# Ten gather buffers in place of six, and products eight slots behind their gathers, in the second group's layers

## The chip, the cores and the metric

The kernel runs on one core of a Trainium2 chip. The metric is the device time of one execution in microseconds, taken as the median of several runs. The core has five engines that run lists of instructions side by side: TensorE (PE in the profile, with its weight loads as PEld), VectorE (DVE), ScalarE (ACT), GpSimd (POOL) and SyncE (SP, which only issues transfers here). Data moves between memory and the core's buffers over 16 DMA engines, which all queues share.

## The reference

512 tokens of width 1024 go through five layers and a feed-forward part with experts ("peer"), all in float32:

```python
x = x + rmsnorm(mamba2_mixer(rmsnorm(x)))        # then sliding-window attention, a hybrid of
...                                              # delta rule and mLSTM, and cross attention
def peer_ffn(h, wq, sub_keys, u_table, v_table):
    q = (hf @ wq).reshape(t, PEER_HEADS, 2, PEER_HALF)
    sc = jnp.einsum('thpd,hpnd->thpn', q, sub_keys).astype(jnp.float32)
    top_v, top_i = lax.top_k(sc, PEER_TOPK)
...
    def block(args):
        xb, eb, gb = args
        u = jnp.take(u_table, eb, axis=0)
        act = jax.nn.gelu(jnp.einsum('phkd,pd->phk', u, xb).astype(jnp.float32), approximate=False)
        wgt = (gb * act).astype(v_table.dtype)
        return jnp.einsum('phk,phkd->pd', wgt, jnp.take(v_table, eb, axis=0))
```

Every token picks 8 x 16 = 128 of 16384 experts. An expert is one row of 1024 numbers in `u_table` and one in `v_table`. The chosen rows of u are multiplied with the token and summed, which gives 128 activations; the rows of v, weighted by these, are added to the token. At the end there is one more norm.

## The kernel before

The tokens are worked on in two groups of two blocks of 128 tokens. Group 0 goes through the five stages `mamba`, `swa`, `hybrid`, `cross` and `route` first (until about 780 us); `route` gives each of its tokens the list of 128 experts. Then group 1 goes through the same five stages, and its own experts are computed densely: `dense` builds a matrix of gates (`gate_matrix`) and then runs 128 steps over all 16384 experts, 128 at a time (`steps`). A word, `phase`, says where the program is in group 1: "B" in the four layers `mamba` to `cross`, "R" in `route`, "G" while the gates are built, "D" in the 128 steps.

Beside group 1's work, group 0's experts are done row by row. The class `Rows` holds a list of 512 gathers: for each of the two blocks 128 of u and then 128 of v. One gather is an indirect DMA that GpSimd issues (L1946): it fetches, for each of the 128 tokens of a block, one row of a table, into a buffer `gu` of 128 x 1024 numbers (512 KB). There are six such buffers (GBUF). `take()` makes the product that belongs to a gather on VectorE: for u, `gu` times the token, summed into one column of `act` (L1967); for v, `x` plus `gu` times a column of `act` (L1973). The products follow their gathers in a list `pend`: `next(lag)` issues a gather and, if more than `lag` are pending, one product. So with a lag of five a product stands five slots behind its gather.

Slots come from the main work. `run()` lets the main work pass from point to point, and at each point adds a rate (1.0 in "B" for `mamba`, 1.1 for the other layers, 0.5 in "R" and "G"); whenever the sum reaches one, the generator `after()` calls `rows.next(GLAG)` with a lag of five. In the dense steps `steps()` itself calls `rows.next(LAGD)`, with LAGD = 3, at a rate that uses up all that is left by the fifth step from the end. `behind()` ties each gather and product to the last matmul so far, for the order of instructions alone; it adds no waiting.

When the last product of a block has been made, `final()` norms the block: a square on ScalarE (L1856), a load of the norm's weights that ScalarE's queue issues (L1860), a product on VectorE (L1862) and the store, again from ScalarE's queue (L1863). For group 0 it stands in `ends`, and each call of `next` runs one half of it; what is left is run after the 128 steps by `drain()`. Group 1's two blocks come after that.

Two more tiles bear on the change. Layers of group 0 hold the low parts of split operands in a tile `hl` (pool `hp`) and a tile `ol` (pool `op`), each 128 x 2 x 1024 numbers or as large. In the layers of group 1 the products are made in full float32 without a split, so neither is in use there; `dense()` takes `hl` again at its start.

In a layer of group 1 the weights come over SP's queue (L359) into three tiles each of `wraw`, `whi` and `wlo`, and TensorE multiplies (L404, transposes L412). VectorE adds the evacuated parts to x (L646, L656), norms x (L500) and makes the products of the gathers between, all in the order of its list.

Of the kernel before, what the change touches and what calls it, by code (L numbers as in the profile page):

```python
# [9 lines left out]
F32 = mybir.dt.float32  # L10
# [10 lines left out]
D = 1024  # L21
# [138 lines left out]
GBUF = 6  # L160
HP = 99
WV = (2, 3)
GLAG = 5
GLEAD = 2
GD = 2.9
GU = 0.75
# [20 lines left out]
class Kern:  # L187
# [72 lines left out]
    @staticmethod  # L260
    def weave(main, side, ratio):
        acc = 0.0
        for _ in main:
            yield
            acc += ratio
            while side is not None and acc >= 1:
                acc -= 1
                if next(side, 0) == 0:
                    side = None
        if side is not None:  # L270
            for _ in side:
                yield
# [1138 lines left out]
    @staticmethod  # L1411
    def weave_keep(main, side, ratio):
        acc = 0.0
        for _ in main:
            yield
            acc += ratio
            while acc >= 1:
                acc -= 1
                next(side, 0)
# [289 lines left out]
    def gate_matrix(self, G, gd, gt):  # L1709
# [7 lines left out]
        acc = 0.0  # L1717
        for s in range(-GLEAD, n + 2):
            if 0 <= s - 2 and s % 2:
# [3 lines left out]
            if 0 <= s - 1 < n:  # L1723
# [5 lines left out]
                nc.scalar.copy(st[:, :, t0 % 8:t0 % 8 + 4, :], q4(p[:, :, 32:128]))  # L1729
            m = s + GLEAD  # L1730
            if m < n:
# [19 lines left out]
            while acc >= 1:  # L1751
                acc -= 1
                next(self.plain, 0)
# [162 lines left out]
    def after(self, gi, x, nb):  # L1916
        yield from self.tail
        self.tail = None
        self.rows = Rows(self, gi, x, nb, self.routed)
        while self.rows.seq:  # L1920
            self.rows.next(GLAG)
            yield
        self.rows.drain()


class Rows:
# [9 lines left out]
    def next(self, lag):  # L1936

        k = self.k
        if self.ends:
            if next(self.ends[0], 0) == 0:  # L1940
                self.ends.pop(0)
        if self.seq:
            b, v, s = self.seq.pop(0)
            t = k.gp.tile([128, D], F32, name="gu", tag="gu", bufs=GBUF)
            table = k.a["p_v" if v else "p_u"]
            self.behind(k.nc.gpsimd.indirect_dma_start(out=t, out_offset=None, in_=table,  # L1946
                                                       in_offset=bass.IndirectOffsetOnAxis(ap=self.res[b][0][:, s:s + 1], axis=0)))
            self.pend.append((b, v, s, t))
            if len(self.pend) > lag:
                self.take()  # L1950
        elif self.pend:
            self.take()

    def behind(self, inst):

        k = self.k
        if k.phase not in "GD":
            k.tc.add_manual_dep(inst.ins, k.last.ins.name, mybir.DependencyInfo(
                mybir.DependencyClass.NoSync, mybir.DependencyReason.SCHED_ONLY), reason="spread over the products")
# [97 lines left out]
```

## Time and profile before

| | us |
|---|---|
| Median of three runs | 2600.91 (2598.08 to 2602.4) |
| The profiled execution | 2595.71 |
| Its span in the profile | 2593.7 |
| TensorE busy | 2376.1 (92%) |
| TensorE weight loads busy | 2134.6 (82%) |
| VectorE busy | 1987.4 (77%) |
| ScalarE busy | 1170.7 (45%) |
| GpSimd busy | 1077.3 (42%) |

The shares are means over stages with different limits: a busy share says little of what one edit is worth, so the stages are looked at apart. The granted clock of TensorE is 0.963 of full speed on the mean. The queue of the gathers (software_dynamic) carried 268 MB of 642 MB. In the chain of work that ended last, TensorE has 60% of the span, VectorE 20%, GpSimd 6% and transfers 5%.

### The profile page before, as it was taken

The page shows a single profiled execution, that of the slowest core. Times are in us where ns is not written, and L with a number is a line of the kernel's source. Part 1 is how long each engine was busy: PE and PEld are TensorE (multiplying, and loading weights), DVE is VectorE, ACT ScalarE, POOL GpSimd, SP SyncE. Part 2 cuts the span into 40 slices and gives each one's busy share as a digit, 9 for nine tenths or more (in the row PEclk, how much of TensorE's full clock was granted, in tenths as well). Part 3 has the DMA queues.
Part 4 walks back from the last instruction along what each step waited for, and adds up shares of the span by engine and source line. Part 5 has one row for each costly group of instructions (what it writes and reads, how often), then busy time and mean ns, then how long its engine had stood idle before and what let it go on. Part 6 is the DMA issues. An engine that isn't in the chain of part 4 may idle for free.

```text
span 2593.7 us, 41054 instructions
## 1 busy us (share of the span) xinstructions
PE 2376.1 (92%) x14872; PEld 2134.6 (82%) x14872; DVE 1987.4 (77%) x3989; ACT 1170.7 (45%) x2406; POOL 1077.3 (42%) x910
## 2 busy tenths in 40 slices
PE   7999998998989899979799859999769999999997
PEld 7999898998988788868678848888658999999974
DVE  7787657757589887877698786794997777777776
ACT  6766566644545433333252312222565444444443
POOL 1112001231011776753568775324335555555552
PEclk9999999999989899989899979999999999999999
DMA  6555434325446999986888689877888888888874
GB/s 203 178 172 156 148 118 142 116 89 150 141 131 197 352 380 358 341 297 224 336 308 302 226 324 353 288 236 282 249 237 302 316 311 286 319 317 300 294 276 152
DMA packets 203962, 642.33 MB, mean 248 GB/s; under 512 B 21104, under 2 KB 53360, under 8 KB 202480
## 3 DMA queue, kind: packets, MB, share of 16 engines
q1 hardware_dynamic: 97216, 347.19, 40.1%
q0 software_dynamic: 73728, 268.47, 28.6%
q10 hardware_dynamic: 32816, 24.06, 2.9%
q8 instruction: 117, 1.92, 0.3%
q14 instruction: 85, 0.70, 0.1%
HBM read 621.74 MB, written 17.89 MB: 247 GB/s over the span
## 4 chain that ended last, share of the span: by engine, by line
PE 60%; DVE 20%; issue 6%; POOL 6%; DMA 5%; ACT 4%; ACTq 0%; POOLq 0%; DVEq 0%; SPq 0%
PE mm L404 37%; PE ax L404 17%; PE tp L404 3%; POOL gu L1946 3%; PE tp L412 2%; DVE x L1973 2%; DVE gu L1967 2%; DMA gu<-in_p_v,eid 2%; DVE wlo L379 2%; DVE cacc L532 1%; DVE o L1736 1%; DMA gu<-in_p_u,eid 1%; DVE q L1738 1%; DVE o L1743 1%; ACT whi L376 1%
## 5 line engine op out<-in xcount | busy, mean ns | idle before, releaser
L379 DVE TENSOR_TENSOR wlo<-wraw,whi 128x1024 fp32r<-128x1024 f32 x285 | 357.2, 1254 | 206.7 <-ACT whi L376 206.4
L1946 POOL DMA_INDIRECT gu<-in_p_v,eid x256 | 367.5, 1436 | 192.4 <-DVE x L1973 111.5
L1946 POOL DMA_INDIRECT gu<-in_p_u,eid x256 | 313.0, 1223 | 273.8 <-DVE gu L1967 171.7
L404 PE MATMUL mm<-hl,whi 128*128 128x256 f32 (+1 forms) x1376 | 392.0, 285 | 0.0
L376 ACT CAST whi<-wraw 128x1024 fp32r<-128x1024 f32 x285 | 298.9, 1049 | 183.9 <-PE mm L404 86.6
L1967 DVE SCALAR_TENSOR_TENSOR gu<-gu,hf 128x1024 f32<-128x1024 f32 x256 | 318.4, 1257 | 45.4 <-DMA gu<-in_p_u,eid 45.0
L1973 DVE SCALAR_TENSOR_TENSOR x<-gu,act,x 128x1024 f32<-128x1024 f32 x256 | 335.3, 1310 | 14.4 <-DMA gu<-in_p_v,eid 13.4
L404 PE MATMUL mm<-hh,whi 128*128 128x260 f32 (+1 forms) x1232 | 331.9, 345 | 2.7 <-DVE spp L563 1.5
L404 PE MATMUL mm<-hh,wlo 128*128 128x260 f32 (+1 forms) x1200 | 320.9, 340 | 4.1 <-DVE wlo L379 4.1
L404 PEld LDWEIGHTS mm<-hl,whi 128*128 128x128 f32 x1376 | 262.7, 191 | 5.0
L1809 POOL TENSOR_TENSOR w<-act,w 128x256 fp32r<-128x256 f32 x128 | 146.4, 1144 | 281.9 <-issue 218.1
L404 PEld LDWEIGHTS mm<-hh,whi 128*128 128x128 f32 x1232 | 237.4, 195 | 22.7 <-ACT hh L510 2.8
L404 PEld LDWEIGHTS mm<-hh,wlo 128*128 128x128 f32 x1200 | 232.8, 196 | 21.5 <-DVE wlo L379 5.0
L404 PE MATMUL mm<-dhh,wlo 128*128 128x256 f32 x752 | 211.7, 282 | 0.0
L404 PE MATMUL mm<-dhh,whi 128*128 128x256 f32 x752 | 209.8, 279 | 0.0
L404 PE MATMUL mm<-wlo,hh 128*128 128x256 f32 x656 | 176.6, 329 | 0.0
L404 PE MATMUL mm<-whi,hh 128*128 128x256 f32 x608 | 166.8, 328 | 0.4 <-ACT hh L510 0.4
L404 PE MATMUL mm<-whi,oh 128*128 128x256 f32 x560 | 147.5, 328 | 1.3 <-DVE ysb L646 1.1
L404 PE MATMUL mm<-hh,wraw 128*128 128x256 f32 (+1 forms) x608 | 147.1, 390 | 0.3 <-ACT act L1706 0.3
L1804 ACT CAST w<-act 128x256 fp32r<-128x256 f32 x128 | 52.2, 408 | 206.9 <-DVE act L1802 204.7
L404 PEld LDWEIGHTS mm<-dhh,whi 128*128 128x128 f32 x752 | 141.1, 188 | 4.0
L404 PEld LDWEIGHTS mm<-dhh,wlo 128*128 128x128 f32 x752 | 141.3, 188 | 0.0
(494 smaller groups left out, 5646.6 us busy)
## 6 DMA issues: line engine op xcount, KB each, us to landing
wraw<-in_w SPq DMA_DIRECT2D x238, 512.0 KB, 4.0
wraw<-in_p_v SPq DMA_DIRECT2D x78, 512.0 KB, 4.7
wraw<-in_p_ut SPq DMA_DIRECT2D x69, 512.0 KB, 4.6
whi<-in_w SPq DMA_DIRECT2D x55, 512.0 KB, 6.1
wlo<-in_w SPq DMA_DIRECT2D x55, 512.0 KB, 6.2
wrawd<-in_p_v SPq DMA_DIRECT2D x50, 512.0 KB, 4.8
wrawd<-in_p_ut SPq DMA_DIRECT2D x36, 512.0 KB, 4.4
gd<-gst ACTq DMA_DIRECT2D x32, 384.0 KB, 3.6
```

What stands on the lines that cost most here:

```text
L376: nc.scalar.copy(hi, raw)
L379: (nc.gpsimd if le == "P" else nc.vector).tensor_tensor(lo, raw, hi.bitcast(F32), op=ALU.subtract)
L404: inst = self.last = self.nc.tensor.matmul(out, lhsT, rhs, start=start, stop=stop, skip_group_check=True)
L412: return self.nc.tensor.transpose(out, in_, self.ident[:in_.shape[0], :in_.shape[0]])
L532: nc.vector.scalar_tensor_tensor(acc, ps[:, 1 + j:1 + j + gt], w[:, j:j + 1], acc, op0=ALU.mult, op1=ALU.add)
L1736: nc.vector.tensor_tensor(o1, self.iota4.rearrange("p i t -> p t i"), row(self.sTb[:, 0, :]), op=ALU.is_equal)
L1738: nc.vector.tensor_tensor(q, self.iota4, col(self.sTb[:, 1, :]), op=ALU.is_equal)
L1804: nc.scalar.copy(wt[:, 0:gt], act)
L1809: nc.gpsimd.tensor_tensor(wt[:, gt:2 * gt], act, wt[:, 0:gt].bitcast(F32), op=ALU.subtract)
L1946: self.behind(k.nc.gpsimd.indirect_dma_start(out=t, out_offset=None, in_=table, in_offset=bass.IndirectOffsetOnAxis(ap=self.res[b][0][:, s ...
L1967: self.behind(nc.vector.scalar_tensor_tensor(t, t, 1.0, self.hf[:, b, :], op0=ALU.mult, op1=ALU.mult, accum_out=acts[b][:, s:s + 1]))
L1973: self.behind(nc.vector.scalar_tensor_tensor(x[:, b, :], t, acts[b][:, s:s + 1], x[:, b, :], op0=ALU.mult, op1=ALU.add))
```

## The change

In phase "B" the lag is eight instead of five, and the gathers go round ten row buffers: the six `gu` buffers, then the two halves of a tile `hl`, then the two halves of a tile `ol`. Outside of phase "B" a gather takes a `gu` buffer as before. In `next`, `if` becomes `while`, so that as many products are made as it takes to bring the list down to the lag asked for.

```diff
@@ -161,6 +161,7 @@
 GLAG = 5
+DEEP = 8
 GLEAD = 2
...
@@ -1918,7 +1919,7 @@
         while self.rows.seq:
-            self.rows.next(GLAG)
+            self.rows.next(DEEP if self.phase == "B" else GLAG)
             yield
...
@@ -1941,15 +1942,28 @@
             b, v, s = self.seq.pop(0)
-            t = k.gp.tile([128, D], F32, name="gu", tag="gu", bufs=GBUF)
+            t = self.buf()
...
             self.pend.append((b, v, s, t))
-            if len(self.pend) > lag:
+            while len(self.pend) > lag:
                 self.take()
         elif self.pend:
             self.take()
+
+    def buf(self):
+
+        k = self.k
+        r = k.rot("rb", GBUF + 4) if k.phase == "B" else 0
+        if r < GBUF:
+            return k.gp.tile([128, D], F32, name="gu", tag="gu", bufs=GBUF)
+        if r % 2 == 0:
+            if r == GBUF:
+                self.pair = k.hp.tile([128, 2, D], F32, name="hl", tag="hl")
+            else:
+                self.pair = k.op_tile([128, 2, D], "ol", "ol")
+        return self.pair[:, r % 2, :]
```

Since lines are added, a line of the kernel after has a higher number: the gather is L1947, the products are L1981 and L1987, the final norm is L1857 to L1864, and the other lines quoted here are one higher.

GpSimd's list in the first layer of group 1, where the ring of buffers has gone round once, reads thus before. A row gives the line, the output and the inputs with numbers of their tiles, the size, and the counts on other engines' semaphores that the instruction waits for (DMASW0 to DMASW7 are eight semaphores of the gathers' queue).

```order
L1946 DMA gu_10246<-in_p_u,eid_9968 128x1024 [waits DMASW6_49,DVE_49]
L1946 DMA gu_10270<-in_p_u,eid_9968 128x1024 [waits DMASW7_49,DVE_49]
L1946 DMA gu_10284<-in_p_u,eid_9968 128x1024 [waits DMASW0_49,DVE_49]
L1946 DMA gu_10295<-in_p_u,eid_9968 128x1024 [waits DMASW1_49,DVE_49]
L1946 DMA gu_10303<-in_p_u,eid_9968 128x1024 [waits DMASW2_49,DVE_49]
L1946 DMA gu_10321<-in_p_u,eid_9968 128x1024 [waits DMASW3_49,DVE_49]
```

After the change the same place on GpSimd reads:

```order
L1947 DMA gu_10241<-in_p_u,eid_9968 128x1024 [waits DMASW6_49,DVE_49]
L1947 DMA gu_10265<-in_p_u,eid_9968 128x1024 [waits DMASW7_49,DVE_49]
L1947 DMA hl_10279<-in_p_u,eid_9968 128x1024 [waits DMASW0_49]
L1947 DMA hl_10279<-in_p_u,eid_9968 128x1024 [waits DMASW1_49]
L1947 DMA ol_10297<-in_p_u,eid_9968 128x1024 [waits DMASW2_49]
L1947 DMA ol_10297<-in_p_u,eid_9968 128x1024 [waits DMASW3_49]
L1947 DMA gu_10322<-in_p_u,eid_9968 128x1024 [waits DMASW4_49,DVE_49]
```

The gathers stand at the same places; four in ten now go to the halves of `hl` and `ol`, and in each round the waits on VectorE are fewer. The number in a wait's name isn't the product waited for.

VectorE's list at the end of the hybrid layer, where TensorE's last output parts are added to x and the next norm begins, reads thus before:

```order
L646 TENSOR_TENSOR x<-mm,x 128x256
L1967 SCALAR_TENSOR_TENSOR gu,act<-gu,hf 128x1024
L496 TENSOR_REDUCE ns_15326<-xss 128x1
L496 TENSOR_REDUCE ns_15335<-xss 128x1
L1967 SCALAR_TENSOR_TENSOR gu,act<-gu,hf 128x1024
L458 TENSOR_SCALAR nv<-ns_15326 128x1
L458 TENSOR_SCALAR nv<-ns_15335 128x1
L1967 SCALAR_TENSOR_TENSOR gu,act<-gu,hf 128x1024
L500 TENSOR_SCALAR xn<-x,nr 128x512 x4
```

After the change, at the same place on VectorE:

```order
L647 TENSOR_TENSOR x<-mm,x 128x256
L1981 SCALAR_TENSOR_TENSOR gu,act<-gu,hf 128x1024
L497 TENSOR_REDUCE ns_15265<-xss 128x1
L497 TENSOR_REDUCE ns_15274<-xss 128x1
L1981 SCALAR_TENSOR_TENSOR gu,act<-gu,hf 128x1024
L459 TENSOR_SCALAR nv<-ns_15265 128x1
L459 TENSOR_SCALAR nv<-ns_15274 128x1
L1981 SCALAR_TENSOR_TENSOR hl,act<-hl,hf 128x1024
L501 TENSOR_SCALAR xn<-x,nr 128x512 x4
```

The products stand at the same places, but each is that of a gather three slots older, and some read `hl` or `ol`.

ScalarE's list at the end of the program, in the last steps of the dense stage (`w` is a step's weighted activation, `whi` the high part of a weight tile), reads thus before:

```order
L376 CAST whid<-wraw 128x1024
L1804 CAST w<-act 128x256
L376 CAST whi<-wrawd 128x1024
L1804 CAST w<-act 128x256
L376 CAST whi<-wrawd 128x1024
L1804 CAST w<-act 128x256
L376 CAST whi<-wraw 128x1024
L1804 CAST w<-act 128x256
L376 CAST whid<-wraw 128x1024
L1856 ACTIVATE gu,fss<-x 128x1024
L1860 DMA gu<-in_bcw 128x1024
L1856 ACTIVATE gu,fss<-x 128x1024
```

After the change, the same stretch of ScalarE's list:

```order
L1805 CAST w<-act 128x256
L1857 ACTIVATE gu,fss<-x 128x1024
L1861 DMA gu<-in_bcw 128x1024
L377 CAST whid<-wraw 128x1024
L1805 CAST w<-act 128x256
L1864 DMA out<-gu 128x1024
L377 CAST whi<-wrawd 128x1024
L1805 CAST w<-act 128x256
L377 CAST whi<-wrawd 128x1024
L1805 CAST w<-act 128x256
L377 CAST whi<-wraw 128x1024
L1805 CAST w<-act 128x256
```

One square, one load of the norm's weights and one store have moved from behind the last step's casts to between them, four steps ahead of the end. The cause is the `while`: in the dense steps the lag asked for is three, the `if` kept the pending list at five there, and now it is brought to three.

## Rows read from the trace of the kernel before

**Rows 1.** Windows: us; PE, PEld, DVE, ACT, POOL busy; PEclk, DMA share, GB/s

```profile
835.00:1640.00 805.00, 707.18 (x3633) 606.62 (x3632) 639.61 (x1216) 260.90 (x635) 531.36 (x454) 0.92 0.87 319
...
1943.00:2480.00 537.00, 534.77 (x3406) 483.81 (x3405) 421.82 (x388) 258.98 (x387) 288.43 (x196) 1.00 0.87 306
2480.00:2594.00 114.00, 95.55 (x368) 64.59 (x366) 76.35 (x83) 42.77 (x64) 45.49 (x41) 0.95 0.58 199
```

**Rows 2.** Windows of the gathers' line alone: us, GpSimd's busy time and count

```profile
835.00:1640.00 805.00, 406.12 (x334) 0.92 0.87 319
1943.00:2480.00 537.00, 169.96 (x97) 1.00 0.87 306
```

**Rows 3.** Waits, 835 to 1640: who waited for whom: us, times, longest

```profile
POOL gu L1946 <- DVE x L1973: 72.0, 35, 7.7
POOL gu L1946 <- DVE gu L1967: 63.9, 49, 4.0
PE tp L412 <- DVE xn L500: 40.6, 7, 14.1
DVE gu L1967 <- DMA gu<-in_p_u,eid: 35.8, 36, 4.3
PE ax L404 <- DVE m_h L817: 14.4, 7, 4.8
DVE x L1973 <- DMA gu<-in_p_v,eid: 13.4, 19, 3.3
```

**Rows 4.** The gathers' line from 1520 to 1545: their count, and issue to landing

```profile
L1946 POOL DMA_INDIRECT gu<-in_p_u,eid x15: 935/937/1913, 1519.1 to 1544.2; - x15
...
DMA to landing us min/median/max: 6.6/8.8/10.5
```

**Rows 5.** Timeline, 1540 us: start, duration, instruction, [idle before <- releaser]

```profile
1540.57 1.24 DVE L1967 SCALAR_TENSOR_TENSOR gu<-gu,hf 128x1024 f32<-128x1024 f32 x1 [0.29 <-DMA gu<-in_p_u,eid]
...
1541.74 0.41 DVE L646 TENSOR_TENSOR x<-mm,x 128x256 f32<-128x256 f32 x1
...
1542.20 1.22 PE L404 MATMUL mm<-wraw,oh 128*128 128x256 f32 x3 [1.90 <-DVE x L646]
```

**Rows 6.** Timeline: the first and the last of the 13 gaps

```profile
938.31 1.22 DVE L1967 SCALAR_TENSOR_TENSOR gu<-gu,hf 128x1024 f32<-128x1024 f32 x1 [1.16 <-DMA gu<-in_p_u,eid]
...
940.20 0.43 PE L404 MATMUL ax<-xdt,M 128*128 128x64 f32 x2 [2.30 <-DVE M L788]
...
1631.20 1.23 DVE L1967 SCALAR_TENSOR_TENSOR gu<-gu,hf 128x1024 f32<-128x1024 f32 x1 [0.73 <-DMA gu<-in_p_u,eid]
...
1637.21 0.69 PE L412 MATMUL tp<-ident,xn 128*128 128x128 f32 x2 [1.25 <-DVE xn L500]
```

**Rows 7.** Windows, two stretches of the layers, columns as in rows 1

```profile
925.00:950.00 25.00, 20.82 (x107) 18.14 (x105) 21.92 (x47) 6.33 (x16) 20.09 (x16) 0.91 1.00 377
...
1530.00:1545.00 15.00, 12.14 (x48) 9.17 (x47) 11.35 (x21) 2.55 (x10) 7.61 (x9) 0.92 1.03 418
```

**Rows 8.** Timeline of GpSimd: a gather and the state step behind it

```profile
1021.97 1.68 POOL L1946 DMA_INDIRECT gu<-in_p_u,eid  x1 [2.51 <-DVE gu L1967]
...
1025.21 0.62 POOL L816 TENSOR_TENSOR m_h<-m_h,cde 128x256 f32<-128x256 f32 x1
```

**Rows 9.** Timeline of VectorE at the start of the route stage

```profile
1651.09 0.49 DVE L1522 MAX8 tv<-sc 128x8 f32<-128x128 f32 x2 [11.25 <-ACT sc L1570]
```

**Rows 10.** The gathers' line in the dense stage: issue to landing

```profile
DMA to landing us min/median/max: 4.6/6.6/11.3
```

**Rows 11.** Timeline of VectorE in the first dense step

```profile
1952.90 1.28 DVE L1973 SCALAR_TENSOR_TENSOR x<-gu,act,x 128x1024 f32<-128x1024 f32 x1
```

**Rows 12.** Timeline at the end, then the transfers of the norm's weights

```profile
2575.40 1.06 ACT L1856 ACTIVATE gu<-x 128x1024 f32<-128x1024 f32 x1
...
2588.20 1.28 DVE L1862 SCALAR_TENSOR_TENSOR gu<-x,finr,gu 128x1024 f32<-128x1024 f32 x1 [3.22 <-DMA gu<-in_bcw]
...
gu<-in_bcw ACTq DMA_DIRECT2D x5, 512.0 KB, 3.9
```

## The prediction

> **What bounds the kernel now.** I read the busy times by stage first [rows 1]. In the layers of the second group (835 to 1640 us) TensorE is busy 707 of 805 us, so 98 us are idle there; VectorE has 640 us of work and the transfer engines are taken 0.87 of the time. In the dense stage (1943 to 2480) TensorE is busy 534.8 of 537 us: nothing but its own work bounds that part. In the last 114 us it is busy 95.6. The gathers that the change speaks of lie mostly in the first of these stages, 334 of 512, and 97 stand in the dense stage [rows 2].
>
> Then I read what the idle engines of the layers wait for [rows 3]. A gather on GpSimd waits for the product that frees its buffer 72.0 + 63.9 = 135.9 us in all. That is the wait the words of the change name, but GpSimd is busy only 531 of 805 us. VectorE waits for a gather to land 35.8 + 13.4 = 49.2 us in 55 waits. This one can matter, since VectorE runs its list in order and a product that waits holds up whatever stands behind it. A product stands five slots behind its gather; 334 slots in 805 us are 2.4 us each, so five slots are about 12 us on the mean. From 1519.1 to 1544.2 us, though, 15 gathers start [rows 4], one every 1.8 us, and five slots are 9.0 us, while these gathers land after 6.6 / 8.8 / 10.5 us (least, median, most).
>
> What one such wait does is seen at 1540 us [rows 5]. The product at 1540.57 waited 0.29 us for its gather; only then could VectorE add the evacuated part at 1541.74, and TensorE, which needs that buffer, started at 1542.20 after 1.90 us of idleness. I went through all TensorE gaps of over 0.6 us in this stage for those with a VectorE wait for a gather in the 6 us ahead: 13 gaps, 36.9 us together. The first and the last of them are [rows 6]. Taking from each gap no more than the gather waits ahead of it (2.30 us with a wait of 1.64 summed over its 6 us at the first, 1.25 with 0.73 at the last) gives 13.2 us. Six lie outside the stretches where the transfers are full (1.64, 1.55, 0.64, 0.84, 0.94, 0.83: 6.4 us), seven inside (1.06, 0.62, 1.90, 0.59, 0.96, 0.92, 0.73: 6.8 us).
>
> **The change part by part.** The number of gathers, products and matmuls stays; no work is added.
>
> *Eight slots and ten buffers in the layers.* Eight slots at 1.8 us are 14.3 us, over the longest landing of 10.5 us [rows 4]. So a wait for a gather goes wherever the transfer engines have room. Where they have none, depth gives only three transfers ahead, once per stretch. The stretch 1530 to 1545 moves 418 GB/s at a share of 1.03 [rows 7]. I take the 6.4 us outside in full and half of the 6.8 us inside: **-9.8 us**. Bounds: nothing (the gap is then ended by the rest of the chain) and -13.2 by these gaps; -49.2 if every wait counted.
>
> Ten buffers do not give ten gathers in flight: as the listing of GpSimd shows, every gather from the ninth on also waits for one of eight semaphores in rotation, thus for the gather eight before it to have landed. After the change a gather waits for the product of ten before it, which stands two slots earlier; the wait for a product goes from GpSimd and the semaphore's takes part of its place. Eight gathers of 0.52 MB (128 rows of 4 KB) at 418 GB/s take 10.0 us if they had all the rate, so in full stretches the wait may just move from buffer to semaphore. That costs GpSimd nothing it doesn't pay now.
>
> The rate of 418 GB/s also bears on a rule. In the Trainium skill, DMA: Bandwidth & Descriptors, section Bandwidth, the measured rate of one core alone ends at 425 GB/s for large transfers, near the ceiling of its ports; the rows' 418 agrees with it. By that rule the 6.8 us inside full stretches would stay whole, and this term would be -6.4.
>
> *GpSimd's own steps.* A gather that waits holds up the state update behind it: at 1021.97 a gather starts after 2.51 us of waiting for a product, and the state step follows at 1025.21 [rows 8]. TensorE waits for that state 14.4 us in 7 waits [rows 3]. Bounds 0 and -14.4; I take **-1 us**, since the gather's own 1.7 us and the rest of the state's chain stay.
>
> *The clock.* In 925 to 950 and 1530 to 1545 the granted clock reads 0.91 and 0.92, a mean of stretches at 2.4 and some at 1.2 GHz, with TensorE idle for 4.2 and 2.9 us in them [rows 7]. At full clock their busy times would fall by at most 20.82 x 0.09 + 12.14 x 0.08 = 2.8 us. I take **-2 us**, bounds 0 and -2.8.
>
> *Layer boundaries.* TensorE waits 40.6 us in 7 waits for a normed x [rows 3]. That chain is the norm's; I count nothing for it, as its first and longest part follows the last matmul of a layer whatever the gathers do.
>
> *Route stage: a burst.* At the first slot of that stage the `while` brings nine pending down to five: three more products than now, about 3.8 us of VectorE work. VectorE waits 11.25 us for scores at 1651.09 [rows 9], which covers it: **0**. Uncovered it would be +3.8.
>
> *Dense stage: the lag falls to three.* Now the `if` takes one product for each gather, so five stay pending though the dense stage asks for three. The `while` brings it to three: two more products in the first dense slot (1.28 us each, the one there now is [rows 11]), 2.6 us of VectorE ahead of the first splits. VectorE is busy 421.8 of 537 us, so bounds 0 and +2.6; I take **+0.5**. From then on a product follows its gather by three slots of 537/97 = 5.5 us, 16.6 us, against landings of 6.6 in the median and 11.3 at most [rows 10]: no new wait.
>
> *End.* As the pending list is shorter by two, it empties two calls earlier, and the final norm of the first group's last block moves from behind the 128 steps into the last steps. There ScalarE and VectorE alternate in one chain: step's cast, split, next product. The listing of ScalarE shows the square, the load of the norm's weights and the store among the casts. The square is 1.06 us and the norm's product 1.28 us [rows 12], so 2.3 us on that chain; the store, on ScalarE's queue, waits for a norm whose weights take 3.9 us to land [rows 12] where a step is some 3.3 us, another 0.6. The tail loses as much work: the last norm now waits 3.22 us for its weights at 2588.20, and with two norms instead of three behind the last matmul up to 2.3 us go. Net +2.9 - 2.3 = +0.6; I take **+1**, bounds -2.3 (all hidden) and +6.2 (2.3 and the whole 3.9, none back).
>
> Sum: -9.8 - 1 - 2 + 0 + 0.5 + 1 = **-11.3 us**. The profiled execution took 2595.71 us (span 2593.7), so 2584.4 by it. That execution is 0.2% under the median of 2600.91; the same -0.435% of the median gives **2590 us**.
>
> **The rivals.**
>
> *No gain, about 2599 us.* The gaps stay, because they are ended by chains that have other waits just behind, or because the wait is for bandwidth and not for depth. For it: the full stretches at 418 GB/s [rows 7], and that TensorE's gaps in [rows 6] are longer than the waits ahead of them, so something else is in them. Against it: six of the gaps lie where transfers have room. With the full-stretch half whole and half of the other gone it is -3.2 - 1 + 1.5 = -2.7. In this case belong also the eight semaphores: if gathers in flight stay capped where they already are, the change does not do what its ten buffers say.
>
> *The larger gain, about 2576 us.* VectorE's lateness lasts beyond 6 us: a product that waits pushes all later adds and casts, and half of the 49.2 us comes back, -25. For it: 98 us of idle TensorE in the stage [rows 1]. Against: VectorE has slack (640 of 805) and catches up between.
>
> *Slower, about 2607 us.* The lag of three in the dense stage: +2.6 for two products at its start and +6.2 at the end with none given back, against a gain in the layers of 2 us or less: 8.8 - 2 = +6.8. It decides as soon as the layers give back less than 3 us. For it: TensorE has 2 us of idleness in the whole dense stage [rows 1], so whatever delays it there shows. Against: VectorE's slack there.
>
> **How the numbers follow.** Forecast (-6 to -17) 0.43; larger gain 0.17; no gain (-5 to +5) 0.28; slower 0.12. A measurement of this kernel tells about 0.2%, 5.2 us, from no change. Faster takes the first two, 0.60; same 0.28; slower 0.12. The range runs from 2575, the larger gain, to 2604, past the no-gain case: the slower case and a far gain, about 0.15, are left out.
>
> **What would show it.** In the profile after: VectorE's waits for gathers in the layers fall from 49.2 us to under 20, TensorE's busy share in 835 to 1640 rises by some 10 us of shortened stage, the dense stage keeps its 537 us to within 2, the last 114 us keep theirs to within 4. GpSimd's waits for products fall from 135.9 us, and waits on earlier gathers appear instead. The prediction is wrong if those waits fall and the stage keeps its length (then the gaps were other chains'), if they don't fall (bandwidth), or if the dense stage or the tail grows by over 4 us.

## The result and the profile after

The changed kernel takes 2575.65 us in the median of 5 runs (2572.47 to 2576.91); the kernel before, run beside it, 2602.37 us. The ratio is 0.9898, with a 95% interval from 0.9883 to 0.9912: 26.7 us less, where 11 were forecast. The time is at the very edge of the stated range, and it is the rival with the larger gain that came near it. The profiled execution took 2576.12 us (span 2574.4), 19.6 us under the profiled one of before.

The windows of the changed kernel answer to [rows 1]. The columns are us; busy time of PE, PEld, DVE, ACT and POOL with counts; the granted clock; the share of the DMA engines; GB/s. The second row holds the same 3633 matmuls of the layers as the first of [rows 1].

```profile
780.00:835.00 55.00, 52.41 (x279) 45.54 (x278) 52.55 (x261) 31.37 (x62) 4.28 (x5) 0.94 0.54 178
840.00:1620.00 780.00, 691.81 (x3633) 597.30 (x3632) 635.88 (x1208) 260.58 (x633) 531.51 (x455) 0.94 0.88 328
1923.00:2460.00 537.00, 534.77 (x3405) 483.77 (x3405) 424.16 (x390) 258.66 (x387) 288.08 (x196) 1.00 0.86 306
```

The whole gain lies in the layers: 805 us have become 780. TensorE's idle time there is length less busy time: 97.8 us before, 88.2 after, 9.6 less. The other 15.4 us are busy time, 707.2 against 691.8 for the same matmuls: they run faster because the granted clock is higher, 0.94 against 0.92. The trace's record of the clock has TensorE at the lower of its two levels (1.2 and 2.4 GHz) for 121 us of this stage before and 96 us after, and busy for 76 and 49 us of that; with half of these taken off, the two kernels' busy time comes to 669 and 667 us, so the clock accounts for nearly all of the 15.4. Ahead of the stage, before a single gather of the new kind, the changed kernel's clock fell once (0.94 in the first row), and it entered the layers 4.6 us later than the kernel before. That fall is of this execution, and it is why the two profiles lie less than 25 us apart. The dense stage has the same 537 us to the tenth, and what follows it takes 115 us where it took 114.

The waits in the layers answer to [rows 3]; the lines are one higher in the changed kernel. First the waits of TensorE, then, from the view of the gathers' line, what the gathers waited for most, who waited for a gather (us, times), and issue to landing.

```profile
PE tp L413 <- DVE xn L501: 38.3, 7, 14.2
PE ax L405 <- DVE m_h L818: 8.3, 5, 4.8
...
  DVE x L1987: 49.5, 18
...
  DVE ol L1981: 11.4, 10
  DVE hl L1981: 7.5, 8
  DVE gu L1981: 6.9, 10
...
DMA to landing us min/median/max: 4.1/8.2/17.1
```

VectorE's waits for gathers fell from 49.2 us to 25.8, not to under 20 as the prediction had asked; none is left among the products of v. GpSimd's waits for products fell from 135.9 us to 70.8 (the 49.5 us of the row, and 21.3 us for products of u). The gathers themselves land later, 8.2 us in the median where it was 7.1 for the same stage before.

### The profile page after: what moved, and what is told of

It is laid out like the page before. It is cut to its first block, busy times and chain, and to the rows that moved or that the text cites. A ratio compares the mean times of both kernels' runs of the same rounds, so it can differ in the third digit from the quotient of the medians.

```text
span 2574.4 us, 40953 instructions
## 1 busy us (share of the span) xinstructions
PE 2365.7 (92%) x14872; PEld 2127.9 (83%) x14872; DVE 1986.7 (77%) x3989; ACT 1170.7 (45%) x2406; POOL 1076.6 (42%) x910
## 4 chain that ended last, share of the span: by engine, by line
PE 63%; DVE 19%; POOL 6%; issue 5%; DMA 4%; ACT 3%; ACTq 0%; POOLq 0%; DVEq 0%; SPq 0%
PE mm L405 40%; PE ax L405 17%; PE tp L405 3%; PE tp L413 3%; DMA gu<-in_p_u,eid 2%; POOL gu L1947 2%; DVE gu L1981 2%; DVE wlo L380 2%; DVE x L1987 2%; DVE o L1737 1%; DVE cacc L533 1%; DVE o L1744 1%; DVE q L1739 1%; ACT whi L377 1%; DVE wk L1525 1%
## 5 line engine op out<-in xcount | busy, mean ns | idle before, releaser
L1947 POOL DMA_INDIRECT gu<-in_p_v,eid x206 | 307.3, 1492 | 127.4 <-DVE x L1987 69.7
L405 PE MATMUL mm<-hh,whi 128*128 128x260 f32 (+1 forms) x1232 | 337.9, 350 | 2.7 <-DVE spp L564 1.5
L1947 POOL DMA_INDIRECT gu<-in_p_u,eid x174 | 215.8, 1240 | 202.8 <-DVE gu L1981 103.6
L1987 DVE SCALAR_TENSOR_TENSOR x<-gu,act,x 128x1024 f32<-128x1024 f32 x206 | 266.9, 1295 | 1.0
L1981 DVE SCALAR_TENSOR_TENSOR gu<-gu,hf 128x1024 f32<-128x1024 f32 x174 | 219.3, 1270 | 16.5 <-DMA gu<-in_p_u,eid 16.2
```

What stands on the lines that cost most here:

```text
L405: inst = self.last = self.nc.tensor.matmul(out, lhsT, rhs, start=start, stop=stop, skip_group_check=True)
L1981: self.behind(nc.vector.scalar_tensor_tensor(t, t, 1.0, self.hf[:, b, :], op0=ALU.mult, op1=ALU.mult, accum_out=acts[b][:, s:s + 1]))
L1987: self.behind(nc.vector.scalar_tensor_tensor(x[:, b, :], t, acts[b][:, s:s + 1], x[:, b, :], op0=ALU.mult, op1=ALU.add))
```

## The experiments

**A second profile, and what the two halves of the change do.** The kernel before with the `while` alone is, in the layers, the kernel before; so its profile is a second one of that stage.

```diff
-            if len(self.pend) > lag:
+            while len(self.pend) > lag:
```

> The kernel before with nothing but the `while` in place of the `if`, so that only the dense stage's lag falls to three and the final norm moves into the last steps. Expected: within 1 us of the kernel before, about +0.4 us; the layers unchanged. If part of the gain came from the dense stage, it would be over 3 us faster.

It took 2602.06 us, a ratio of 1.0004 (0.9993 to 1.0015): the dense stage and the end gave nothing, as expected. But its layers don't look like those of [rows 1]. The first row is the window of the same matmuls; the others, on VectorE and TensorE, are the end of the hybrid layer:

```profile
833.00:1645.00 812.00, 703.53 (x3630) 602.40 (x3630) 643.03 (x1214) 260.32 (x633) 527.20 (x454) 0.93 0.86 316
...
1553.36 1.23 DVE L1967 SCALAR_TENSOR_TENSOR gu<-gu,hf 128x1024 f32<-128x1024 f32 x1 [1.68 <-DMA gu<-in_p_u,eid]
...
1556.73 1.23 DVE L1967 SCALAR_TENSOR_TENSOR gu<-gu,hf 128x1024 f32<-128x1024 f32 x1 [2.01 <-DMA gu<-in_p_u,eid]
...
1558.52 1.39 PE L412 MATMUL tp<-ident,xn 128*128 128x128 f32 x4 [11.03 <-DVE xn L500]
```

The same instructions took 812 us and left TensorE idle for 108.5, not 97.8. At the layer's end two products, which stand between the steps of the norm, waited 1.68 and 2.01 us for their gathers, and TensorE stood idle for 11.03 us until x was normed. In the profile on which the prediction rests, that gap was 6.08 us, with waits of 0.59 us in all ahead of it. In the changed kernel it is this:

```profile
1532.75 1.23 DVE L1981 SCALAR_TENSOR_TENSOR hl<-hl,hf 128x1024 f32<-128x1024 f32 x1 [0.24 <-DMA hl<-in_p_u,eid]
...
1534.53 1.39 PE L413 MATMUL tp<-ident,xn 128*128 128x128 f32 x4 [6.07 <-DVE xn L501]
```

The gap is not always so in the changed kernel's layers: in the profile of late_store below, which has the same layers, two products between the steps of this norm waited 1.08 and 1.36 us, and TensorE stood idle for 9.68 us.

Next, the buffers without the lag, and the lag with as few buffers as it can run with:

```diff
-DEEP = 8
+DEEP = 5
```

> Ten buffers as in the changed kernel, but a product follows its gather by five slots in the layers, as before. Theory 1 (VectorE waited for gathers that had not landed, and TensorE and its clock behind it; what helps is the distance in slots): the gathers may be issued a little earlier, since GpSimd no longer waits for products, but the products stand as near as before; VectorE's waits for gathers stay above 35 us of the 49.2 before, and under half of the 26.7 us come back: 2590 to 2600 us. Theory 2 (GpSimd was held up 135.9 us by waits for products, and its own steps and TensorE behind them; what helps is the number of buffers): the whole gain, 2574 to 2580 us.

```diff
-        r = k.rot("rb", GBUF + 4) if k.phase == "B" else 0
+        r = k.rot("rb", GBUF + 3) if k.phase == "B" else 0
```

> Lag of eight with nine buffers, the least that this lag can run with: a gather again waits for the product made in the slot just before it, as in the kernel before. Theory 1 (distance in slots): VectorE's waits for gathers stay near the 26 us of the changed kernel, and so does the time, 2574 to 2582 us. Theory 2 (number of buffers frees GpSimd): GpSimd's waits for products return to over 110 us, and most of the gain goes: 2592 to 2602 us.

Ten buffers with lag five took 2590.65 us, 0.9961 of the kernel before beside it (0.9946 to 0.9977); nine with lag eight 2587.63 us, 0.9944 (0.9931 to 0.9957). Neither theory has it: each half alone gives some 10 to 15 us, both together 23 to 27. The windows of the layers, ten with five first:

```profile
833.00:1629.00 796.00, 698.42 (x3632) 600.50 (x3631) 640.25 (x1215) 260.42 (x634) 524.99 (x455) 0.93 0.87 322
```

```profile
834.00:1628.00 794.00, 697.48 (x3632) 601.18 (x3631) 637.35 (x1211) 260.76 (x635) 527.40 (x453) 0.93 0.87 322
```

Both leave TensorE idle for 97 us (97.6 and 96.5), between the 97.8 and 108.5 of the two profiles of before and the 88 to 91 of the four profiles with both halves. VectorE's idle time ahead of products, summed over the layers whatever ended it, is 49 and 52 us in the two profiles of before, 34 with lag five and 24 with nine buffers and lag eight; GpSimd's ahead of gathers (beyond the 0.3 us of an issue) is 135 and 140, 77 and 123. So the buffers free GpSimd and take a third off VectorE's idle time too; the lag takes VectorE's down to 24 to 26 us and gives some of GpSimd's back (94 us in the changed kernel, 77 with lag five).

**The dense stage and the end.**

```diff
-LAGD = 3
+LAGD = 5
```

> The changed kernel with the dense stage's lag set to five, which is what took effect there before: no extra products at its start and the first group's final norm behind the 128 steps again. From the two traces (the last matmul came 3.2 us nearer to the stretch before it in the kernel before, the rest behind it took 2.8 us longer) I expect 0 to 1 us less than the changed kernel: 2574 to 2576 us, the last matmul 3 us earlier, the tail 3 us longer, the dense stage's length the same within 0.2 us. If the burst and the norm cost what the prediction held possible (8.8 us), it would be 2567 us.

It took 2579.65 us on that chip, 0.9916 (0.9900 to 0.9932), so no difference from the changed kernel that times can show. The traces do. From one matmul at the dense stage's start (1953.0 us in the kernel before) to the last matmul it is 625.5 us before, 628.7 in the changed kernel and 625.5 here; from the same matmul to the end of the span 640.6, 641.1 and 640.5. So the move of the norm costs 3.2 us in the loop and gives 2.8 back behind it, some 0.4 net, as expected.

```diff
         nc.vector.scalar_tensor_tensor(o, xb, r, wb, op0=ALU.mult, op1=ALU.mult)
+        yield
         nc.scalar.dma_start(self.out[blk * 128:(blk + 1) * 128, :], o)
```

> The changed kernel with one more stop in the final norm, ahead of its store: the store of the first group's last block goes behind the 128 steps, the square and the product stay in the last steps. In the changed kernel ScalarE waited 2.33 us with the store for VectorE's product, and a cast stood behind it. Expected: the last matmul 2 to 2.5 us nearer to the dense stage's steps, the tail the same within 0.5 us, so about 2 us under the changed kernel, 2573 to 2577 us. If the norm's own work (2.3 us) is what costs, nothing changes.

It took 2572.86 us, 0.9898 (0.9875 to 0.9922): the fastest median of the study, though not told apart from the changed kernel by its time. In the changed kernel the store on ScalarE's queue held a cast up, as the first row shows; with the extra stop the same cast follows its step's cast of `w` without a wait, as the next rows show (kernel with the late store):

```profile
2548.20 1.04 ACT L377 CAST whi<-wrawd 128x1024 fp32r<-128x1024 f32 x1 [2.33 <-DVE gu L1863]
```

```profile
2541.57 0.41 ACT L1805 CAST w<-act 128x256 fp32r<-128x256 f32 x1 [1.88 <-DVE act L1803]
2541.88 1.05 ACT L377 CAST whi<-wrawd 128x1024 fp32r<-128x1024 f32 x1
2545.78 0.41 ACT L1805 CAST w<-act 128x256 fp32r<-128x256 f32 x1 [2.85 <-DVE act L1803]
```

From the matmul at the dense stage's start to the last one it is 627.5 us here, where the changed kernel has 628.7, and to the end of the span 639.8, the least of the four; so 1.2 us came back in the loop and not 2.3, since the casts of `w` in the two steps behind it wait longer for VectorE (2.85 and 2.16 us, and 1.88 in the step ahead).

**All waits between gathers and products away.**

```diff
-        r = k.rot("rb", GBUF + 4) if k.phase == "B" else 0
+        r = k.rot("rb", GBUF + 2) if k.phase == "B" else 0
...
+            o = self.still(t)
+            i0 = self.hf[:, b, :] if o is not t else t
-            self.behind(nc.vector.scalar_tensor_tensor(t, t, 1.0, self.hf[:, b, :], op0=ALU.mult, op1=ALU.mult,
+            self.behind(nc.vector.scalar_tensor_tensor(o, i0, 1.0, self.hf[:, b, :], op0=ALU.mult, op1=ALU.mult,
...
+            i0 = self.hf[:, b, :] if k.phase == "B" else t
-            self.behind(nc.vector.scalar_tensor_tensor(x[:, b, :], t, acts[b][:, s:s + 1], x[:, b, :],
+            self.behind(nc.vector.scalar_tensor_tensor(x[:, b, :], i0, acts[b][:, s:s + 1], x[:, b, :],
...
+    def still(self, t):
...
+        k = self.k
+        if k.phase != "B":
+            return t
+        if not hasattr(self, "scratch"):
+            self.scratch = k.op_tile([128, 2, D], "ol", "ol")[:, 0, :]
+        return self.scratch
```

> In the four layers the products read the block's tokens again instead of the gathered rows, and write a tile of their own: no product waits for a gather there and no gather for a product (eight buffers, only the landing of the last write to each). All gathers and products are still issued at the same places, so the load on VectorE, GpSimd and the DMA engines is the same; the row sums in these layers are left out of the output. It shows what all waits between gathers and products are worth. Of the changed kernel's 26 us of VectorE waits and 71 us of GpSimd waits, if they still hold TensorE up: 2560 to 2570 us. If what remains of TensorE's 88 us of idleness in the layers is the norms' and other chains: 2573 to 2578 us, and then the change has got nearly all there is.

It took 2622.78 us, 1.0092 (1.0068 to 1.0117): slower than the kernel before. Both expectations fall. In the first layer it was indeed ahead: at the matmul that the kernel before starts at 980 us it had won 17 us since 780. It lost that and more in single stretches, of which this is one (window, then TensorE, ScalarE and VectorE):

```profile
1320.00:1340.00 20.00, 10.58 (x37) 7.24 (x37) 7.92 (x22) 3.44 (x7) 14.10 (x14) 0.76 1.03 420
...
1325.85 2.30 PE L405 MATMUL mm<-hh,wraw 128*128 128x260 f32 x9
...
1330.60 0.59 PE L405 MATMUL mm<-hh,wraw 128*128 128x260 f32 x1 [0.83 <-issue]
...
1334.93 0.47 ACT L531 ACTIVATE cacc<-mm,hcw 128x256 f32<-128x256 f32 x1 [12.04 <-remote]
...
1335.44 0.48 DVE L533 SCALAR_TENSOR_TENSOR cacc<-mm,hcw,cacc 128x256 f32<-128x256 f32 x1 [10.92 <-issue]
```

GpSimd, held by no product, issues a gather every 1.24 us; the DMA engines are full at 420 GB/s, and TensorE does a matmul now and then with nothing named that it waits for, while ScalarE and VectorE stand idle for 12 and 11 us behind it. So the wait for a product is not all loss: it spaces the gathers. That the unspaced gathers are what slows the kernel is argued from such stretches and not tested by itself. What starves TensorE there the profile doesn't name (for gathers and weights it gives no time of landing), and it stays open. A weight tile that lands late does not fit: of the sixteen matmul records in a row on one tile, the first nine, at 1325.85, run without a break, and the gaps come behind them.

**The clock by itself.** Matmuls of the identity, read by nobody, at the four layer boundaries, on the changed kernel and on the kernel before, with the changed kernel unaltered beside them:

```diff
+FILL = 32
...
+        if self.phase in "BR" and self.rows is not None and self.layer != "mamba":
+            with self.tc.high_priority(HP):
+                p = self.ps([128, 128], "ax")
+                for _ in range(FILL):
+                    i = nc.tensor.matmul(p, self.ident, self.ident, start=True, stop=True, skip_group_check=True)
...
```

> The changed kernel once more, unaltered, beside the next two on the same chip: a second profile of it. If the sizes read from one profile each (TensorE idle in the layers 97.8 us before and 88.2 after, TensorE at the lower clock 121 us before and 96 after) are of the kernel and not of the execution, this one reads 86 to 92 us idle and 92 to 106 us at the lower clock, at 2572 to 2580 us.

> The changed kernel with 32 matmuls of the identity, whose results nobody reads, on TensorE at each of the four layer boundaries of the second group (swa, hybrid, cross, route), where TensorE sits idle for 10 to 14 us for the next normed x and the granted clock is low for 7 to 24 us behind it. They take the clock term by itself. If TensorE's idleness costs its clock behind it (theory: each us of idleness costs about half a us more in clock), the time at the lower clock in the layers falls from about 100 to under 65 us and the kernel is 12 to 25 us faster than the changed one: 2552 to 2565 us. If the low clock has another cause, or the matmuls delay the norm's transposes as much: 2573 to 2582 us.

> The kernel before with the same 32 matmuls at the same four boundaries, and nothing of the change. If what the clock gives here is independent of the gathers, it gains as much as the changed kernel does by them: 2577 to 2590 us. If the two overlap, the difference between it and the changed kernel with them is under 15 us; if not, it stays at 20 to 27 us.

The unaltered kernel took 2575.07 us, 0.9912 (0.9886 to 0.9937), with TensorE idle for 90.1 us of the layers, as expected, and at the lower clock for 110 us, more than the 92 to 106 expected. With the matmuls it took 2579.97 us, 0.9932 (0.9908 to 0.9956); the kernel before with them 2601.43 us, 1.0013 (0.9994 to 1.0032). So they gained nothing, and the two stay 21 us apart. The time at the lower clock in the layers was 92 us in both: a little less than in the changed kernel, far from the 65 expected, and well under the 121 and 119 of the kernel before. The mean granted clock did rise, from 0.965 to 0.968 in the unaltered kernel's runs to 0.969 to 0.972, and from 0.960 to 0.966 to 0.965 to 0.970 in the kernel before. Behind the boundary of swa, the changed kernel first, the one with the matmuls second (its profile is of the slowest of its five runs, 2588.7 us):

```profile
1104.00:1125.00 21.00, 8.76 (x37) 6.87 (x38) 11.84 (x45) 8.23 (x21) 9.13 (x13) 0.59 0.55 189
```

```profile
1104.00:1125.00 21.00, 12.55 (x85) 10.74 (x84) 13.80 (x48) 5.99 (x19) 12.36 (x15) 0.79 0.70 236
```

The clock of that stretch went from 0.59 to 0.79, but mostly where TensorE has no work of its own. The lower clock still reached 6.6 us past the first transpose of the normed x (it ends at 1126.3 us, the transpose starts at 1119.7), and 6.4 us without the matmuls; and from the last matmul of the layer to the same matmul some 40 further on it is 27.7 us with them and 27.6 without. At the start of the route stage 6.8 us at the lower clock did go altogether, yet the same distance there was 16.7 us with them and 15.2 without: there and at cross they stood among the norm's transposes (at cross the next layer's first matmul followed the last of them at once). So the lower clock goes with TensorE's idleness, and work in its place can take it away, as in the route stage; that time can be bought back so is not shown.

**How far ahead GpSimd may run.** Lag and buffers were set one by one around the changed kernel.

```diff
-DEEP = 8
+DEEP = 7
```

> The changed kernel with a lag of seven in place of eight, ten buffers: a gather waits for a product made three slots earlier, and a product follows its gather by seven slots. The runs so far: lag five with ten buffers 2590.7, lag eight with nine 2587.6, both against 2602.2 of before, the changed kernel 0.990 of before. If distance and free buffers help one another (theory 3), this has a slot less of the one and a slot more of the other: within 4 us of the changed kernel, 2574 to 2582 us. If distance alone decides (theory 1), it is a third of the way back: 2583 to 2588 us.

```diff
-DEEP = 8
+DEEP = 9
```

> Ten buffers with a lag of nine: the distance grows by a slot, but a gather waits again for the product made in the slot just before it. Theory 3 (distance and free buffers together): GpSimd's waits for products go from 71 us back over 95 us and the time rises, 2582 to 2590 us. Theory 1 (distance alone): no slower than the changed kernel, under 2577 us.

```diff
-DEEP = 8
+DEEP = 7
...
-        r = k.rot("rb", GBUF + 4) if k.phase == "B" else 0
+        r = k.rot("rb", GBUF + 3) if k.phase == "B" else 0
```

> Nine buffers, lag seven: GpSimd may run two slots ahead of the products, as in the changed kernel, with one buffer and one slot of lag less. Theory 4 (buffers less lag decides, two is best): faster than both its neighbours, under 2584 us, where nine buffers with lag 8 took 2587.6 and ten with lag 7 took 2590.1. Theory 5 (lag and buffers each help by themselves): slower than either neighbour, 2588 to 2596 us.

> Ten buffers, lag seven, once more, on the chip of the other two. If its loss against the changed kernel is of the kernel: 0.993 to 0.997 of the kernel before, and in the profile again stalls of several us around the stretches at a DMA share of 1.03 (TensorE's gap of 4.1 us at the end of swa). If it was of that execution or chip: 0.989 to 0.992.

```diff
-DEEP = 8
+DEEP = 6
```

> Ten buffers, lag six: four slots ahead. Theory 4: no better than lag seven, 2588 to 2596 us. Theory 5: between lag five (2590.7) and lag seven (2590.1) or, if these two are noise about a line to lag eight, 2583 to 2588 us.

All settings together, with the idle time of VectorE ahead of products, of GpSimd ahead of gathers and of TensorE in the layers of each one's profile (one execution, where the ratio is that of all runs):

| Buffers, lag | ratio (95% interval) | VectorE, us | GpSimd, us | TensorE, us |
|---|---|---|---|---|
| 6, 5 (two profiles) | 1 | 49, 52 | 135, 140 | 97.8, 108.5 |
| 10, 5 | 0.9961 (0.9946 to 0.9977) | 34 | 77 | 97.6 |
| 10, 6 | 0.9943 (0.9922 to 0.9963) | 27 | 72 | 98.1 |
| 10, 7 | 0.9955 (0.9933 to 0.9978) | 23 | 90 | 100.3 |
| 10, 7 again | 0.9923 (0.9904 to 0.9941) | 26 | 93 | 91.7 |
| 10, 8 | 0.9898 (0.9883 to 0.9912) | 26 | 94 | 88.2 |
| 10, 8 again | 0.9912 (0.9886 to 0.9937) | 22 | 104 | 90.1 |
| 10, 9 | 0.9933 (0.9908 to 0.9959) | 22 | 121 | 97.1 |
| 9, 7 | 0.9932 (0.9915 to 0.9949) | 30 | 105 | 96.1 |
| 9, 8 | 0.9944 (0.9931 to 0.9957) | 24 | 123 | 96.5 |

In time, ten buffers took 2585.75 us with lag six, 2590.10 and 2579.82 with lag seven and 2584.80 with lag nine, nine buffers with lag seven 2582.49. The kernel before took 2601.99 us beside the first run of lag seven and lag nine and 2598.74 beside the other three, so the ratios compare better. Lag nine came out as theory 3 has it (GpSimd's waits for products back at 114 us), the first run of lag seven as neither theory has it. Nine buffers with lag seven came within the range of theory 4 and ten with lag six within that of theory 5, so these two are not decided.

Lag seven was between 0.990 and 0.998 on two chips; the gap of 4.1 us at the end of swa, which its first profile had and its second hadn't, was of the execution. From lag five to eight the ratio falls, and at nine, where a gather again waits for the product of the slot before, GpSimd's waits and the ratio rise, though the intervals of the ratio touch. The sums of the waits do not give this order: lag six has the least of both together and gained only about half. What goes with the ratio is TensorE's own idleness, so it counts where a wait falls. In the profile of lag six one product between the norm's steps at the end of the hybrid layer waited 5.05 us for its gather, and TensorE stood idle for 16.01 us there, against 6.07 in the changed kernel. That two slots between buffers and lag were best of themselves is not shown: nine buffers with lag seven come out no better than ten with lag seven, and the intervals touch.

## Why the prediction was right and wrong

**The sum's places were right.** The gain is in the layers alone. The dense stage's start cost 0.1 us where 0.5 was taken (the matmul at 1940 us of before is 19.8 us earlier, that at 1960 us 19.7). The burst in the route stage cost nothing that shows: VectorE waits 8.46 us for scores behind it in the changed kernel. At the end the loop lost 3.2 us and the tail won 2.8, where 2.9 and 2.3 had been worked out. GpSimd's state step gave a few us where 1 had been counted: TensorE's waits for it were 14.4 and 16.6 us in the two profiles of before, and 8.3, 13.5, 14.0 and 9.8 in the four of the changed layers. The fall to 8.3 in the first is partly luck: there and in late_store a gap of over 4 us at 940 us is put down to another tile.

**The term of the gaps: right in one pair of profiles, somewhat small for the kernel.** It was -9.8 us and the pair of profiles shows 9.6 us less idleness. But only about half of it came at the 13 gaps that were listed: they went from 36.9 us to 32.0. Of the six outside full stretches four went or shrank (0.84, 1.30, 0.83 to nothing; 2.33 to 1.00), the one at 940 us grew from 2.30 to 4.27; of the seven inside, the gap of 1.90 us at 1542, shown in [rows 5] as the example, was still there with 2.21. The rest came from gaps that the list had left out, as they had no wait in the 6 us ahead: 13.72 to 12.39 at the hybrid layer's start, 1.70 at 1026 and 0.68 at 1365 to nothing. (For `mixed` a gap went from 11.41 to 9.67, but the one ahead of it grew from 1.28 to 2.92.)

One profile of before was also taken for the kernel. Its execution was 6.7 us under the median, and the text carried that over as a ratio of the whole; the second profile of the same layers took 812 us and not 805, with 108.5 us of idleness. There are two profiles of these layers before and four with ten buffers and lag eight. From the same matmul to the same matmul:

| | length, us | TensorE idle | TensorE busy | at the lower clock |
|---|---|---|---|---|
| Before (before, before_while) | 805, 812 | 97.8, 108.5 | 707, 704 | 121, 119 |
| Changed (after, after_again, dense_lag5, late_store) | 780, 786, 785, 782 | 88.2, 90.1, 87.9, 91.1 | 692, 696, 697, 691 | 96, 110, 105, 95 |

On the means the layers lost 25 us: 14 of idleness, where the terms of the gaps and of GpSimd's steps were 10.8 together, and 11 of busy time, where the term of the clock was 2.

**The layer boundaries were counted at nothing, and shouldn't have been.** The text said that the norm's chain goes on whatever the gathers do. Products stand within that chain on VectorE, as the listing ahead of the prediction shows, and when they wait for gathers the chain does: 11.03 us against 6.07 above. That pair is the far end of it: TensorE's waits for a normed x were 40.6 and 48.4 us in all in the two profiles before, and 38.3, 38.2, 38.1 and 42.0 in the four after, some 5 us less on the means, of the 14.

**The step that failed is the term of the clock.** It was -2 us, with 2.8 as its bound, worked out from two stretches of 40 us together in a stage that reads 0.92 over 805 us; the bound left out what the other 765 us lose. Over all timed executions the mean granted clock is 0.9633 for the kernel before (58) and 0.9662 for the changed one (10). Taking the time lost as one less the clock, times the length, gives 95.4 and 87.0 us: an estimate of 8.4 us of the 25 between their means, so a third. The profiles agree: half of the time for which TensorE was busy at the lower clock in the layers is 38 and 33 us before, and 24, 29, 31 and 24 after, so 8.6 us less on the means. A stretch where it is plain (before first, then after, the same part of the first layer):

```profile
974.80:1035.20 60.40, 56.37 (x279) 49.62 (x279) 46.72 (x90) 18.58 (x48) 41.89 (x36) 0.92 0.97 368
```

```profile
978.40:1030.50 52.10, 51.10 (x279) 45.61 (x278) 45.40 (x88) 18.57 (x47) 40.35 (x36) 1.00 1.02 406
```

Before, TensorE was idle for 4 us in it, in gaps of 2.33 and 1.70 us, and the clock fell to its lower level behind each; after, with one gap of 1.00 us, it didn't fall. So 3 us less of idleness came with 5.3 us less of busy time. A gap of that length doesn't always bring it: in late_store the same stretch had a gap of 2.29 us and the clock stayed at 1.00. What decides it no run here tells apart.

**The rivals.** The larger gain gave the time (2576), and its account holds in part: VectorE's waits fell by 23.4 us, near the 25 that it let come back, and gaps with no such wait in the 6 us ahead shrank too. But TensorE's idleness fell by 14 us on the means and not by 25; the rest is the clock, of which that rival knew nothing. That its number came out is partly luck. The eight semaphores did not make the ten buffers idle: GpSimd waited on earlier gathers for only 8.2 us in the layers. No gain for want of bandwidth fell too: the transfers ran fuller, 406 GB/s where it was 368 above, and 328 against 319 over the stage. The 425 GB/s that the Trainium skill gives as one core's measured rate for large transfers (DMA: Bandwidth & Descriptors, Bandwidth) was not passed, 420 being the most in the stretches shown here; but that the waits in full stretches would stay whole, as the prediction drew from it, holds only for some: those seven gaps lost 2.8 us in the pair, of the 6.8 that were priced. Slower by the end and the dense stage fell with before_while, at 1.0004.

## What to carry to other kernels

A gap on the engine that bounds is worth more than its length where the clock falls behind it: price the clock over the whole stage and not over the stretches one has looked at. Of a stage whose waits hang on how transfers fall, one profile is one draw; set it against the median first, and take a second profile of the same code where one can. A sum of waits on a helping engine does not rank kernels; look at which of them stand in front of the engine that bounds. Buffers and distance serve two engines, one the issuer of the transfers and one their reader, and a pipeline deepened in only one of them got about half.

## What the runs showed that was not expected

Waits of the issuer space the transfers, and that can be worth more than it costs. With none of them, the kernel was 0.9% slower than the one with 136 us of them: gathers every 1.24 us, the DMA engines full at 420 GB/s, TensorE down to a matmul now and then with no releaser named, and VectorE and ScalarE at a stand for up to 12 us at a time.
